# A hybrid encoder layer with retrieval on one core: gates from contiguous one-hots, output and query by pairs of tiles, and other tiles taken densely

## The chip, the cores and the metric

The kernel runs on one core of a Trainium2 chip. The metric is the device time of one execution in microseconds; runs are compared by their medians. Engines are named as in the profile: PE is TensorE, PEld its weight loads, DVE VectorE, ACT ScalarE, POOL GpSimd (it issues the gathers), SP SyncE (it issues the other transfers).

## The reference, cut to what matters

One layer over 1024 tokens of 1024 channels: modulation from a conditioning vector, an input projection, chunked band attention (8 heads of 64) beside a gated delta rule (4 heads of 128, a state carried from chunk to chunk), an output projection, and a retrieval of single-neuron experts. The last part decides most of the time:

```
qry = rms_norm((hb @ w_query).reshape(128, 8, 256), query_gain)
s1, s2 = scores of the two halves of qry against 128 sub-keys each
v1, i1 = top_k(s1, 16); v2, i2 = top_k(s2, 16)
top_s, pos = top_k(v1[..., :, None] + v2[..., None, :], 16)
experts = i1 * 128 + i2 at pos              # 8 heads x 16 of 16384 experts
gates = softmax(top_s)
act = gelu(einsum(expert_down[experts], hb))
y = einsum(gates * act, expert_up[experts])
```

## The kernel before, in words

The 1024 tokens are eight tiles of 128. For each tile the front does a projection (`project`, lane P, for groups of one or two tiles, `GROUPS`), the delta rule (`delta`, lane D, one tile behind the other by the state), attention (`attention`, lane M), the output projection with the second norm, the query and its top 16 (`output`, lane O), the choice of experts (`choose`, lane R) and, for dense tiles, the gates (`gates_dense`, lane G). A scheduler orders the instructions of each engine by the lanes' priorities (`PRI`, `STEP` a tile, `SHIFT` by hand) and by its own idea of time; each engine then runs its list in order. What a lane may hold in flight is set by its rings of buffers (`RINGS`, `WBUFS`) and PSUM banks (`BANKS`).

The experts are served in two ways. For a **dense** tile (`DENSE`) every expert is computed: the gates are spread to a table of 128 x 128 experts for each token (`gates_dense` builds one-hots of the two keys and multiplies them on PE), and `dense` runs over all experts in 32 steps of four blocks, with products split in a high and a low part. For a **sparse** tile (`SPARSE`) the 128 chosen rows of each token are gathered: `down` issues 128 indirect gathers of 128 x 1024 and a dot product on DVE for each (L893, L895), `up` another 128 with a multiply-add (L907, L912). Each gather goes into a row buffer of a ring: three in the front (`NROW`), and four more when the dense stage's pools are opened (`NMORE`). `FRONT` says behind which tile's front work a sparse tile's rows are put in, `LATE` which tiles' rows go in beside the dense stage; rows have a low priority. The dense stage's pools take the memory of the front's lanes.

Of the kernel before, what the change touches and what calls it, by code (L numbers as in the profile page):

```python
# [50 lines left out]
BANKS = {"P": 2, "D": 2, "M": 1, "O": 1}  # L51
RINGS = {'P': 4, 'D': 12, 'M': 4, 'O': 3, 'R': 2, 'G': 6}
XBUFS = {'P': 1, 'O': 1}
# [3 lines left out]
SPREAD = {('P', 0): 'PR', ('P', 1): 'PR', ('O', 6): 'ORR', ('D', 0): 'DDO'}  # L57
# [5 lines left out]
SHIFT = {('P', 7): -4000, ('P', 5): 5000, ('R', 0): -5000, ('O', 0): -3000, ('O', 7): -13000, ('M', 5): -5000, ('D', 1): 2000, ('O', 6): 11000, ('P', 0): 5000, ('D', 3): -2000, ('R', 3): -3000, ('R', 4): -10000, ('D', 6): 3000, ('M', 4): 2000, ('D', 5): 5000, ('R', 6): 10000, ('G', 5): 1000, ('R', 1): -10000}  # L63
OLANE = {7: 'P'}
ONV = ''
# [57 lines left out]
def hybrid_layer(ctx, tc, a, out):  # L123
# [385 lines left out]
    def attention(t, mixT):  # L509
# [3 lines left out]
        for p in range(4):  # L513
# [9 lines left out]
            for hh in range(2):  # L523
# [3 lines left out]
                for lo, hi, bias in ((m0, 3, farm[:, min(m0, 2) * P:]), (max(m0, 3), 5, near[:, hh, (max(m0, 3) - 3) * P:])):  # L527
# [159 lines left out]
    def output(t, mixT):  # L687
        x = x4("x1")
        SP.dma_start(x, a["x"][rows_(t)])
        for nb in range(2):  # L690
            ps = natural(mixT, [t], "w_out", nb)[t]
            cs = slice(nb * 512, (nb + 1) * 512)
            tmp = rg()
            gate_row(tmp, 0, cs)
            V.tensor_tensor(tmp, ps, tmp, OP.mult)
            V.tensor_tensor(x[:, cs], x[:, cs], tmp, OP.add)
            yield
        h2T = lt([P, KD, P], F, "h2T", 1, "h2T" if cur[0] == "O" else "hT")
        SP.dma_start(x1d[rows_(t)], x)
        norm_T(x, h2T, 0, a2, sh2)  # L700
        yield
        if t in DENSE:
            SP.dma_start(h2Td[DENSE.index(t)], h2T)
        else:
            h2 = x4("h2")
            for q in range(2):
                ps = mm()
                for j in range(4):
                    PE.transpose(ps[:, j * P:(j + 1) * P], h2T[:, 4 * q + j, :], ident)
                A_.activation(h2[:, q * 512:(q + 1) * 512], ps, AF.Copy)  # L710
            SP.dma_start(h2d[rows_(t)], h2)
        yield
        nb = 2 if cur[0] == "O" else 1
        v12 = lt([P, 16, TOPK], F, "v12", nb)
        i12 = lt([P, 16, TOPK], U32, "i12", nb)
        ssq = lt([P, PH], F, "ssq", nb)
        for blk in range(4):
            (_, _, ps), = transposed(h2T, P, "peer_w_query", blk, 4)
            q, sq = rg(), rg()
            A_.activation(sq, ps, AF.Square)  # L720
            for c in range(2):
                A_.activation(q.rearrange("p (a c n) -> p c a n", c=2, n=P)[:, c],
                              ps.rearrange("p (a c n) -> p c a n", c=2, n=P)[:, c], AF.Copy, scale=qgain[:, c:c + 1])
            yield
            pq = mm()
            for cc in range(4):
                PE.matmul(pq[:, cc // 2:cc // 2 + 1], sq[:, cc * P:(cc + 1) * P], ones_col, start=(cc % 2 == 0),
                          stop=(cc % 2 == 1), skip_group_check=True)
            V.tensor_copy(ssq[:, 2 * blk:2 * blk + 2], pq[:, 0:2])
            ps = mm()  # L730
            for cc in range(4):
                PE.matmul(ps[:, cc * P:(cc + 1) * P], q[:, cc * P:(cc + 1) * P], skT[:, cc % 2, :], start=True, stop=True,
                          skip_group_check=True)
            sc_ = copy(ps)
            for cc in range(4):
                top16(sc_[:, cc * P:(cc + 1) * P], P, v12[:, 4 * blk + cc, :], i12[:, 4 * blk + cc, :])
                yield
        TOP[t] = v12, i12, ssq
# [11 lines left out]
    def choose(t):  # L750
# [39 lines left out]
        e12 = lt([P, 2, PH, TOPK], F, "e12", 2)  # L790
# [37 lines left out]
        ROUTE[t] = (idx, idf.rearrange("p h s -> p (h s)"), gt.rearrange("p h s -> p (h s)"))  # L828
        yield


# [238 lines left out]
```

## Time and profile before

| | |
|---|---|
| median of 3 runs | 3556.13 us (3547.57 to 3564.26) |
| the profiled execution | 3552.79 us |
| its span, first to last instruction | 3551.0 us |
| mean granted TensorE clock | 0.914 of full speed |
| busy: PE, DVE, POOL, ACT | 3131.2, 2797.2, 1281.6, 1029.7 us |
| moved by DMA | 1029.12 MB, 290 GB/s |

The busy times are unions of what an engine had in work; matmuls overlap each other, so a busy PE isn't a full one. Shares over the span mix three stages with different limits, so stretches are read apart below. Nothing runs beside another core.

### The profile page before, as it was taken

Reading aid. Unit: us, or ns where it says so; the run is one execution under the profiler, and the core shown is the slowest. Engines: PE = TensorE matmul, PEld = TensorE weight load, DVE = VectorE, ACT = ScalarE, POOL = GpSimd, SP = SyncE. Lnnn points to the kernel's source line nnn. Section 1 sums busy time; section 2 is a strip of 40 time slices with the busy share of each in tenths; the row PEclk is TensorE's granted clock in tenths of the full one; section 3 lists DMA queues with packets and bytes.
Section 4 is the critical chain, followed back from the end, with each engine's and each line's share of the span. In section 5 each row is a group of like instructions: output and inputs, shape, how many; then the busy total and the mean of one; then the engine's idle time right before and its main releaser. Section 6 shows DMA issues by size and latency. Waiting matters only on the chain.

```text
span 3551.0 us, 46244 instructions
## 1 busy us (share of the span) xinstructions
PE 3131.2 (88%) x16220; PEld 2603.9 (73%) x16220; DVE 2797.2 (79%) x6626; ACT 1029.7 (29%) x1809; POOL 1281.6 (36%) x1028
## 2 busy tenths in 40 slices
PE   6888789899989899999856999999989999999990
PEld 4678678788778788788755777777777777777870
DVE  3346577877876886656688888999989888999899
ACT  2233243234423343232212322222222222222220
POOL 0000333222222330000232446666655655665455
PEclk9999889998889899987878999999999999999995
DMA  8865789887787897543787989999999998999889
GB/s 280 280 215 170 256 298 315 298 284 246 241 289 244 274 323 247 196 144 133 268 283 254 313 301 342 338 355 355 355 333 351 340 334 318 352 362 367 311 276 356
DMA packets 382602, 1029.12 MB, mean 290 GB/s; under 512 B 34576, under 2 KB 135312, under 8 KB 382368
## 3 DMA queue, kind: packets, MB, share of 16 engines
q0 software_dynamic: 147456, 536.94, 42.1%
q1 hardware_dynamic: 234912, 489.23, 40.3%
q8 instruction: 127, 2.08, 0.2%
q14 instruction: 107, 0.88, 0.1%
HBM read 964.16 MB, written 61.87 MB: 289 GB/s over the span
## 4 chain that ended last, share of the span: by engine, by line
DVE 14%; PE 12%; DMA 10%; issue 10%; POOL 4%; ACT 1%; DVEq 0%; POOLq 0%; ACTq 0%; SPq 0%
PE yc L993 5%; PE at L971 5%; DMA g<-gd 4%; DVE row L895 4%; DVE y L912 3%; POOL row L893 3%; DMA row<-in_peer_expert_down_dram,idx 3%; DMA rawd<-_peer_expert_down_t_dram 2%; DVE ulo L953 1%; DVE yacc L998 1%; DVE dlo L953 1%; POOL row L907 1%; DVE gl L977 1%; DMA row<-in_peer_expert_up_dram,idx 1%; PE mm L364 1%
## 5 line engine op out<-in xcount | busy, mean ns | idle before, releaser
L893 POOL DMA_INDIRECT row<-in_peer_expert_down_dram,idx x512 | 646.5, 1263 | 1489.1 <-DVE idx L827 411.3
L907 POOL DMA_INDIRECT row<-in_peer_expert_up_dram,idx x512 | 634.9, 1240 | 754.8 <-DVE y L912 314.3
L895 DVE CUSTOM_DVE_ANT_0 row<-row,h2a 128x1024 f32<-128x1024 f32 x512 | 620.2, 1217 | 122.0 <-DMA row<-in_peer_expert_down_dram,idx 121.3
L912 DVE SCALAR_TENSOR_TENSOR y<-row,act,y 128x1024 f32<-128x1024 f32 x508 | 649.4, 1278 | 11.6 <-DMA row<-in_peer_expert_up_dram,idx 8.6
L993 PE MATMUL yc<-uhi,whi 128*128 128x512 f32 x1024 | 397.2, 400 | 32.2 <-ACT whi L980 24.4
L993 PE MATMUL yc<-ulo,whi 128*128 128x512 f32 x1024 | 402.0, 396 | 14.6 <-DVE ulo L953 14.5
L993 PE MATMUL yc<-uhi,wlo 128*128 128x512 f32 x1024 | 370.9, 396 | 7.1 <-DVE wlo L981 6.9
L971 PE MATMUL at<-hhi,dhi 128*128 128x512 f32 x1024 | 269.2, 405 | 72.6 <-ACT dhi L952 46.4
L971 PEld LDWEIGHTS at<-hhi,dhi 128*128 128x128 f32 x1024 | 195.3, 194 | 128.3 <-ACT dhi L952 88.0
L364 PE MATMUL mm<-h2T,w 128*128 128x128 f32 x2048 | 272.6, 292 | 17.1 <-DMA w<-in_peer_w_query_dram 7.3
L364 PEld LDWEIGHTS mm<-h2T,w 128*128 128x128 f32 x2048 | 265.3, 207 | 26.6 <-DMA w<-in_peer_w_query_dram 8.5
L870 PE MATMUL mm<-rg 128*128 128x128 f16 x1024 | 263.1, 411 | 7.5 <-ACT stg L873 6.3
L993 PEld LDWEIGHTS yc<-uhi,whi 128*128 128x128 f32 x1024 | 195.9, 192 | 85.8 <-ACT whi L980 32.3
L971 PE MATMUL at<-hlo,dhi 128*128 128x512 f32 x1024 | 258.7, 394 | 0.0
L971 PE MATMUL at<-hhi,dlo 128*128 128x512 f32 x1024 | 255.1, 389 | 0.0
L350 PE MATMUL mm<-w,hT 128*128 128x256 f32 x1024 | 243.2, 389 | 1.4 <-ACT raw L441 0.9
L993 PEld LDWEIGHTS yc<-ulo,whi 128*128 128x128 f32 x1024 | 195.7, 191 | 58.7 <-DVE ulo L953 18.2
L993 PEld LDWEIGHTS yc<-uhi,wlo 128*128 128x128 f32 x1024 | 195.3, 191 | 50.2 <-DVE wlo L981 9.7
L971 PEld LDWEIGHTS at<-hlo,dhi 128*128 128x128 f32 x1024 | 196.6, 192 | 42.1
L971 PEld LDWEIGHTS at<-hhi,dlo 128*128 128x128 f32 x1024 | 192.3, 188 | 40.0
L350 PEld LDWEIGHTS mm<-w,hT 128*128 128x128 f32 x1024 | 194.7, 196 | 28.9 <-ACT raw L441 1.1
L870 PEld LDWEIGHTS <-rg 128*128 128x128 f16 x1024 | 146.8, 147 | 78.1 <-issue 8.0
(294 smaller groups left out, 4914.9 us busy)
## 6 DMA issues: line engine op xcount, KB each, us to landing
w<-in_w_in_dram SPq DMA_DIRECT2D x140, 512.0 KB
w<-in_peer_w_query_dram SPq DMA_DIRECT2D x128, 512.0 KB
rawd<-_peer_expert_down_t_dram SPq DMA_DIRECT2D x128, 512.0 KB
rawu<-in_peer_expert_up_dram SPq DMA_DIRECT2D x128, 512.0 KB
w<-in_w_out_dram SPq DMA_DIRECT2D x64, 512.0 KB
gd<-stg SPq DMA_DIRECT2D x64, 512.0 KB
g<-gd SPq DMA_DIRECT2D x32, 1024.0 KB
w<-in_w_ada_dram SPq DMA_DIRECT2D x48, 512.0 KB
```

The source lines that it names most:

```text
L350: PE.matmul(ps[t][:, hf * 256:hf * 256 + 256], hT[:, k, tt * P:(tt + 1) * P], w[k], start=(k == 0), stop=(k == KD - 1), skip_group_check=True)
L364: PE.matmul(ps[:, (c % per) * W:(c % per + 1) * W], w[k][:, (c % 2) * P:(c % 2 + 1) * P], hT[:, k, :W], start=(k == 0), stop=(k == KD - 1) ...
L870: PE.matmul(ps[:, j * P:(j + 1) * P], w[n][:, :, 4 * h + j], oh1[:, :, 4 * h + j], start=(n == 0), stop=(n == GN - 1), skip_group_check=True)
L893: G.indirect_dma_start(out=r, out_offset=None, in_=a["peer_expert_down"], in_offset=bass.IndirectOffsetOnAxis(ap=idx[:, j:j + 1], axis=0))
L895: V.tensor_tensor_reduce(r, r, h2, 1.0, 0.0, OP.mult, OP.add, accum_out=act[:, j:j + 1])
L907: G.indirect_dma_start(out=row, out_offset=None, in_=a["peer_expert_up"], in_offset=bass.IndirectOffsetOnAxis(ap=idx[:, j:j + 1], axis=0))
L912: V.scalar_tensor_tensor(y, row, w[:, j:j + 1], y, op0=OP.mult, op1=OP.add)
L953: V.tensor_tensor(lo, x, hi.bitcast(F), OP.subtract)
L971: PE.matmul(ps, l[:, k, :], r[:, k, :], start=(n == 0), stop=(n == 3 * KD - 1))
L977: V.tensor_tensor(gq, gq, gt[q][:, :, (s % 2) * SCN + c, :], OP.mult)
L993: PE.matmul(ps, l[:, ts_], r[:, cs], start=(m == 0), stop=(m == 3 * SCN - 1))
L998: V.tensor_tensor(yacc[:, n, cs], yacc[:, n, cs], ps, OP.add)
```

## The change

Five things, in one edit. (1) The dense tiles are 2 to 5 instead of 1 to 4, so the sparse ones are 0, 1, 6 and 7; rows of tiles 0 and 1 go into the front, rows of 6 and 7 beside the dense stage (before: 0 in the front, 5 to 7 in `LATE`). (2) `GROUPS` are four pairs, and `output` works on a pair: both tiles share each load of w_out and peer_w_query, and the query's matmuls are 256 columns wide. (3) The gates' one-hots lie token by token in memory instead of eight tokens side by side, and the weighting by the gate moves from DVE (one multiply over eight tokens) to ACT (a scaled copy for each token and part). (4) A query block's attention scores are one matmul over up to three key blocks. (5) The level masks and `iota_n` take less memory, lanes D and O get a second bank, and the hand-set shifts are gone.

```diff
-DENSE = (1, 2, 3, 4)
-FRONT = {0: [('d', 0), ('u', 0)]}
-LATE = [('d', 5), ('u', 5, 1), ('d', 6), ('u', 6, 1), ('d', 7), ('u', 7)]
+DENSE = (2, 3, 4, 5)
+FRONT = {0: [('d', 0)], 1: [('u', 0, 1), ('d', 1), ('u', 1)]}
+LATE = [('d', 6), ('u', 6, 1), ('d', 7), ('u', 7)]
...
 NROW = 3
 NMORE = 4
...
-XBUFS = {'P': 1, 'O': 1}
+XBUFS = {'P': 1, 'O': 2}
...
-BANKS = dict(P=2,D=1,M=1,O=1,R=1)
-GN = 2
+BANKS = dict(P=2, D=2, M=1, O=2, R=1)
 GQ = 8
-GT = mybir.dt.bfloat16 if GN == 3 else BF
-GROUPS = [[0], [1, 2], [3, 4], [5, 6], [7]]
+GROUPS = [[0, 1], [2, 3], [4, 5], [6, 7]]
...
-                    for m in range(lo, hi):
-                        PE.matmul(ps[:, (m - lo) * P:(m - lo + 1) * P], kv[hp, 0, :], kv[hp, 1 + m, :], start=True,
-                                  stop=True, skip_group_check=True)
+                    PE.matmul(ps[:, :(hi - lo) * P], kv[hp, 0, :],
+                              kv[hp, 1 + lo:1 + hi, :].rearrange("p m c -> p (m c)"), start=True, stop=True,
+                              skip_group_check=True)
...
-    def output(t, mixT):
+    def output(tiles, mixT):
+        W = len(tiles) * P
...
-            (_, _, ps), = transposed(h2T, P, "peer_w_query", blk, 4)
+            for c0, per, ps in transposed(h2T, W, "peer_w_query", blk, 4):
...
-                oh1, oh2 = hot(), hot()
-                V.tensor_tensor(oh1, iota_n, spread_(0), OP.is_equal)
-                V.tensor_tensor(oh2, iota_n, spread_(1), OP.is_equal)
-                w = [hot() for _ in range(GN - 1)] + [oh2]
-                for n in range(GN):
-                    V.tensor_tensor(w[n], oh2, spread_(2 + n), OP.mult)
+                oh1, oh2, whi, wlo = (rg((P, GQ * P), BF).rearrange("p (n i) -> p n i", n=GQ) for _ in range(4))
+                for oh, key in ((oh1, 0), (oh2, 1)):
+                    V.tensor_tensor(oh, iota_n[:, None, :].to_broadcast([P, GQ, P]),
+                                    keys[:, key, n0:n0 + GQ, None].to_broadcast([P, GQ, P]), OP.is_equal)
                 for h in range(GQ // 4):
                     ps = mm()
                     for j in range(4):
-                        for n in range(GN):
-                            PE.matmul(ps[:, j * P:(j + 1) * P], w[n][:, :, 4 * h + j], oh1[:, :, 4 * h + j],
-                                      start=(n == 0), stop=(n == GN - 1), skip_group_check=True)
+                        n = 4 * h + j
+                        for m, w in enumerate((whi, wlo)):
+                            A_.activation(w[:, n, :], oh2[:, n, :], AF.Copy, scale=parts[:, m, n0 + n:n0 + n + 1])
+                            PE.matmul(ps[:, j * P:(j + 1) * P], w[:, n, :], oh1[:, n, :], start=(m == 0),
+                                      stop=(m == 1), skip_group_check=True)
...
-            mixT = pools_["O"].tile([P, KD, P], F, name="mixT", tag="mixT", bufs=2)
-            lane("D", when("D", t), run, delta(t, mixT), tile_=t)
-            lane("M", when("M", t), run, attention(t, mixT), tile_=t)
-            with tc.issue_after(first_loads) if t == 0 else ExitStack():
-                lane(OLANE.get(t, "O"), when("O", t), run, output(t, mixT), tile_=t)
+        with tc.issue_after(first_loads) if n == 0 else ExitStack():
+            lane("O", when("O", g[0]), run, output(g, mixT), tile_=g[0])
```

What the scheduler made of it is seen at three places. The first is GpSimd's list from its first gather, before (L893 gathers down rows, L907 up rows; a count stands at the end of a row):

```order
L893 DMA row<-in_peer_expert_down_dram,idx 128x1024 x128
L907 DMA row<-in_peer_expert_up_dram,idx 128x1024 x128
L893 DMA row<-in_peer_expert_down_dram,idx 128x1024 x56
L907 DMA row<-in_peer_expert_up_dram,idx 128x1024
L893 DMA row<-in_peer_expert_down_dram,idx 128x1024
```

And the same list of the change, from where the up rows of tile 1 stand; ahead of it are tile 0's 128 down rows, and then its up rows and tile 1's down rows by turns, 128 of each:

```order
L907 DMA row<-in_peer_expert_up_dram,idx 128x1024 x128
L893 DMA row<-in_peer_expert_down_dram,idx 128x1024 x100
L907 DMA row<-in_peer_expert_up_dram,idx 128x1024
L893 DMA row<-in_peer_expert_down_dram,idx 128x1024 x5
L907 DMA row<-in_peer_expert_up_dram,idx 128x1024
```

Where tile 0's 256 gathers were followed by tile 5's, now 512 of tiles 0 and 1 come ahead of any of tile 6.

The second place is VectorE's list at the start of the dense stage, before (hlo is the low part of the dense tiles' input; L742 to L746 are top 16 searches of the last tile):

```order
L743 MAX_INDEX pos<-tv,rg 128x8
L742 MAX tv<-rg 128x8
L772 COPY d_15265<-i_15263 128x8
L745 MAX tv<-wk 128x8
L773 TENSOR_TENSOR d_15265<-i_15263 128x8x15
L944 TENSOR_TENSOR hlo<-hraw,hhi 128x8x128
```

And of the change, from the last up rows of tile 1 (L912) to their gate and residual (L919, L920); hlo stands some fifty rows further down, and no row pass of tiles 0 and 1 behind it:

```order
L912 SCALAR_TENSOR_TENSOR y<-row,act,y 128x1024
L790 SCALAR_TENSOR_TENSOR b__15793<-pf 128x128
L805 TENSOR_TENSOR rg<-pf,tab_280 128x1024
L787 CAST m_15791<-pw 128x128
L805 TENSOR_TENSOR rg<-pf,tab_280 128x1024
L827 TENSOR_REDUCE s_15868<-gt 128x8
L309 TENSOR_SCALAR s_15996<-ssq 128x8
L912 SCALAR_TENSOR_TENSOR y<-row,act,y 128x1024
L810 TENSOR_TENSOR rg<-rg,d_15786 128x256 x2
```

The third place is the gates of one tile, before, on VectorE (L861 and L862 compare for the one-hots, L865 weights them, L912 is a row pass, L624 one of the delta rule):

```order
L912 SCALAR_TENSOR_TENSOR y<-row,act,y 128x1024 x2
L861 TENSOR_TENSOR rg<-iota_n,gparts 128x1024
L862 TENSOR_TENSOR rg<-iota_n,gparts 128x1024
L729 COPY ssq<-mm 128x2
L865 TENSOR_TENSOR rg<-rg,gparts 128x1024
L309 TENSOR_SCALAR s_8504<-ssq 128x8
L624 TENSOR_TENSOR rg<-rg,kc 128x512
L865 TENSOR_TENSOR rg<-rg,gparts 128x1024
```

And of the change on ScalarE, where each L869 is one token's scaled one-hot, L873 takes four tokens' products out of PSUM, and L538 and L579 belong to attention and the delta rule:

```order
L869 ACTIVATE rg<-rg,gparts 128x128 x15
L538 ACT_TABLE_LOAD
L538 ACTIVATE sx,s_10682<-sx,s_10690 128x640
L873 ACTIVATE stg<-mm 128x128x4
L538 ACTIVATE sx,s_10682<-sx,s_10700 128x640
L869 ACTIVATE rg<-rg,gparts 128x128 x2
L873 ACTIVATE stg<-mm 128x128x4
L869 ACTIVATE rg<-rg,gparts 128x128 x6
```

The weighting has left VectorE's list; 1024 such copies stand in ScalarE's, between the chains of attention and the delta rule, and TensorE's gate matmuls each read one of them.

## Rows read from the trace of the kernel before

**Rows 1.** Stretches: time, then busy us (x instructions) by engine, clock, DMA.

```profile
core 0: us, PE busy (x) PEld busy (x) DVE busy (x) ACT busy (x) POOL busy (x), PEclk, DMA share, GB/s
0.00:371.00 371.00, 310.74 (x2010) 252.28 (x2011) 168.91 (x745) 113.75 (x255) 3.35 (x7) 0.93 0.68 229
371.00:812.00 441.00, 394.41 (x2325) 347.52 (x2325) 333.58 (x1082) 153.87 (x323) 132.72 (x127) 0.91 0.85 297
...
1711.00:1884.00 173.00, 124.01 (x811) 115.61 (x810) 131.86 (x519) 35.10 (x78) 62.20 (x55) 0.79 0.82 281
0.00:1915.00 1915.00, 1683.88 (x10076) 1435.47 (x10076) 1314.90 (x4639) 616.47 (x1286) 345.28 (x319) 0.88 0.74 252
1915.00:3465.00 1550.00, 1447.36 (x6144) 1168.47 (x6144) 1404.69 (x1925) 413.28 (x524) 889.28 (x664) 0.98 0.93 333
3465.00:3551.00 86.00, 0.00 (x0) 0.00 (x0) 77.58 (x64) 0.00 (x0) 47.00 (x46) 0.50 0.93 361
```

**Rows 2.** DVE's row passes alone in such stretches: busy us (x passes).

```profile
core 0: us, DVE busy (x), PEclk, DMA share, GB/s
371.00:812.00 441.00, 154.96 (x128) 0.91 0.85 297
...
0.00:1915.00 1915.00, 386.60 (x312) 0.88 0.74 252
1915.00:3465.00 1550.00, 807.02 (x661) 0.98 0.93 333
3465.00:3551.00 86.00, 66.00 (x52) 0.50 0.93 361
```

**Rows 3.** Timeline from 1763 us, start and duration: DVE's down rows, one gather.

```profile
1763.69 1.21 DVE L895 CUSTOM_DVE_ANT_0 row<-row,h2a 128x1024 f32<-128x1024 f32 x1
...
1765.17 0.94 POOL L893 DMA_INDIRECT row<-in_peer_expert_down_dram,idx  x1 [3.64 <-DVE v L745]
...
1772.99 1.22 DVE L895 CUSTOM_DVE_ANT_0 row<-row,h2a 128x1024 f32<-128x1024 f32 x1 [1.03 <-DMA row<-in_peer_expert_down_dram,idx]
```

**Rows 4.** Row tiles in 1711 to 1884 us; gathers and waits in 371 to 812.

```profile
L895 DVE CUSTOM_DVE_ANT_0 row<-row,h2a x56: 1198/1220/1227, 1710.6 to 1883.4; 128x1024 f32<-128x1024 f32 x56
...
DMA to landing us min/median/max: 4.1/7.0/10.0
...
  DVE act L895: 131.6, 50
...
DMA to landing us min/median/max: 4.2/7.2/10.6
...
DVE row L895 <- DMA row<-in_peer_expert_down_dram,idx: 67.0, 39, 5.5
```

**Rows 5.** By line: key scores (PE) in 300 to 345, 560 to 665; idx.

```profile
L732 PE MATMUL mm<-peer_sub_keys,rg x16: 273/275/276, 309.0 to 328.3; 128*128 128x128 f32 x16
...
L732 PE MATMUL mm<-peer_sub_keys,rg x32: 272/275/421, 562.2 to 659.6; 128*128 128x128 f32 x32
...
L827 DVE CAST idx<-idf x4: 205/217/220, 365.1 to 1931.6; 128x128 int32<-128x128 f32 x4
```

**Rows 6.** PE's timeline: fp32 products at 56, dense ones at 2300, dense start.

```profile
58.80 2.48 PE L364 MATMUL mm<-hT,w 128*128 128x128 f32 x20
...
2299.91 0.39 PE L993 MATMUL yc<-uhi,wlo 128*128 128x512 f32 x1
2300.14 0.39 PE L993 MATMUL yc<-uhi,whi 128*128 128x512 f32 x1
...
1915.70 0.80 PE L971 MATMUL at<-hhi,dhi 128*128 128x512 f32 x1 [26.03 <-DVE hlo L944]
```

**Rows 7.** Groups by line and form: busy, mean ns, idle before.

```profile
L870 PE MATMUL mm<-rg 128*128 128x128 f16 x1024 | 263.1, 411 | 7.5 <-ACT stg L873 6.3 <-DVE rg L865 0.7 <-DVE s L314 0.3
...
L865 DVE TENSOR_TENSOR rg<-rg,gparts 128x1024 f16<-128x1024 f16 x128 | 86.9, 683 | 0.5
...
L796 DVE TENSOR_TENSOR rg<-pf,tab 128x1024 f16<-128x1024 f16 x16 | 19.4, 1215 | 0.0
...
L670 ACT ACTIVATE rg<-rg,e 128x128 f32<-128x128 f32 x96 | 33.4, 394 | 11.4 <-PE mm L327 10.2 <-DVE s L314 1.2
```

**Rows 8.** Timeline of the end.

```profile
3542.36 4.62 DVE L1006 TENSOR_TENSOR x1c<-x1c,yacc 128x1024 f32<-128x1024 f32 x4
```

More of the change, by code (lines that the diff above doesn't have):

```diff
@@ L684, in delta_side @@
         yield
-    def output(t, mixT):
-        x = x4("x1")
-        SP.dma_start(x, a["x"][rows_(t)])
+    def output(tiles, mixT):
+        W = len(tiles) * P
+        xs = []
+        for t in tiles:
+            xs.append(x4("x1"))
+            SP.dma_start(xs[-1], a["x"][rows_(t)])
         for nb in range(2):
-            ps = natural(mixT, [t], "w_out", nb)[t]
+            ps_ = natural(mixT, tiles, "w_out", nb)
             cs = slice(nb * 512, (nb + 1) * 512)
[L693 to L696, printed above, removed]
-            yield
[L698 to L706, printed above, removed]
-                ps = mm()
[L708 to L717, printed above, removed]
-            (_, _, ps), = transposed(h2T, P, "peer_w_query", blk, 4)
[L719 to L738, printed above, removed]
@@ new lines, in output @@
+            g1 = rg()
+            gate_row(g1, 0, cs)
+            for t, x in zip(tiles, xs):
+                tmp = rg()
+                V.tensor_tensor(tmp, ps_[t], g1, OP.mult)
+                V.tensor_tensor(x[:, cs], x[:, cs], tmp, OP.add)
+            yield
+        h2T = lt([P, KD, 256], F, "h2T", 1)
+        for tt, (t, x) in enumerate(zip(tiles, xs)):
+            SP.dma_start(x1d[rows_(t)], x)
+            norm_T(x, h2T, tt, a2, sh2)
+            yield
+            own = h2T[:, :, tt * P:(tt + 1) * P]
+            if t in DENSE:
+                SP.dma_start(h2Td[DENSE.index(t)], own)
+            else:
+                h2 = x4("h2")
+                for q in range(2):
+                    ps = mm()
+                    for j in range(4):
+                        PE.transpose(ps[:, j * P:(j + 1) * P], own[:, 4 * q + j, :], ident)
+                    A_.activation(h2[:, q * 512:(q + 1) * 512], ps, AF.Copy)
+                SP.dma_start(h2d[rows_(t)], h2)
+            yield
+            TOP[t] = (lt([P, 16, TOPK], F, "v12", 2), lt([P, 16, TOPK], U32, "i12", 2), lt([P, PH], F, "ssq", 2))
@@ L823, in choose @@
             return
-        idf = keep.tile([P, PH, TOPK], F, name="idf", tag="idf")
+        idf = lt([P, PH, TOPK], F, "idf", 1)
         V.scalar_tensor_tensor(idf, e12[:, 0], 128.0, e12[:, 1], op0=OP.mult, op1=OP.add)
@@ L1039, in hybrid_layer @@
             lane("P", ADAP, run, ada_rest())
-        for t in g:
-            mixT = pools_["O"].tile([P, KD, P], F, name="mixT", tag="mixT", bufs=2)
-            lane("D", when("D", t), run, delta(t, mixT), tile_=t)
-            lane("M", when("M", t), run, attention(t, mixT), tile_=t)
-            with tc.issue_after(first_loads) if t == 0 else ExitStack():
-                lane(OLANE.get(t, "O"), when("O", t), run, output(t, mixT), tile_=t)
+        mixT = pools_["O"].tile([P, KD, 256], F, name="mixT", tag="mixT", bufs=1)
+        for tt, t in enumerate(g):
+            own = mixT[:, :, tt * P:(tt + 1) * P]
+            lane("D", when("D", t), run, delta(t, own), tile_=t)
+            lane("M", when("M", t), run, attention(t, own), tile_=t)
+        with tc.issue_after(first_loads) if n == 0 else ExitStack():
+            lane("O", when("O", g[0]), run, output(g, mixT), tile_=g[0])
+        for t in g:
             lane("R", when("R", t), run, choose(t), tile_=t)
```

78 lines of the change are left out of this document (49 added, 29 removed).

## The prediction

> **What bounds the kernel now.** I read the busy time by stretches first, then the sparse row passes in the same stretches, then what one row waits for, then the dense stage and the tail. The program falls into three parts [rows 1]: a front of 1915 us (projections, delta rule, attention, output and query, routing, gates), a dense stage from 1915 to 3465 us, and a tail of 86 us. In the dense stage TensorE is the bound: it has 6144 matmuls that follow each other at 0.227 us [rows 6], so 1395 us at the least of 1550; VectorE is busy 1405 of the 1550 and DMA 93% of it, both close behind. In the tail TensorE is idle, and 52 row passes are worked off [rows 1, 2].
>
> The front is tied to TensorE (1684 of 1915 us busy), with VectorE at 1315. The sparse tiles' row passes lie in it as filling. Their count is what matters here: 312 of the 1024 stand ahead of the dense stage [rows 2]. One row is a gather of 512 KB into one of three buffers (NROW) and one VectorE pass. The reader is to see in [rows 3] how one buffer turns: a pass starts at 1763.69 and lasts 1.21, the buffer's next gather is issued at 1765.17, and the pass on it starts at 1772.99, held up by its DMA: 9.3 us, in which each of the three buffers turns once. A gather lands a median 7.0 to 7.2 us after its issue [rows 4]. So three rows take some 1.2 + 0.3 to the issue (the two starts in [rows 3] are 1.48 apart) + 7.0 + about 0.4 to the next pass = 8.9 us, 2.97 us a row, however idle the engines are. What the stretches show: 128 down rows in 441 us, 3.45 a row, with VectorE busy 76% and TensorE 89%; 56 rows in 173 us, 3.09 a row, with VectorE 76% and TensorE 72% [rows 1, 2]. In the dense stage four more buffers are there, and 661 rows take 1550 us, 2.34 a row, beside everything else.
>
> **The change, part by part.**
>
> *Four sparse tiles, now two and two.* Ahead of the dense stage 512 rows stand in VectorE's order instead of 312, and hlo, which the first dense matmul needs, stands behind them all. All 512 go through the same three buffers, since NROW is unchanged and the four further buffers come only with the dense pools; two streams that alternate (up of tile 0, down of tile 1) share them.
>
> When can the first row go? The key scores of tile 0 end at 328 us and of tile 1 at 660, and tile 0's idx stands at 365 [rows 5], 37 us behind. Weighing each matmul in the orders by its columns at the trace's pace, TensorE has 309 us of work up to the first of these and 570 to the second; in the changed order the pair 0, 1 has its last key scores at 463. Interpolated: 328 + (463 - 309) / (570 - 309) x 332 = 524 us; with 37 us, and 14 us for a second tile's selections in between, the first row is at 575 us (540 to 610).
>
> Then 512 rows. Bounds: 2.97 us each by the cycle above, 3.45 by the d-row stretch. I take 3.15, nearest to the 56 rows, because the changed front has less TensorE work beside its rows, as that stretch had: 512 x 3.15 = 1613 us. From the last row of a stretch to the first dense matmul it was 1883.4 to 1915.7 [rows 4, 6], 32 us; I take 30. The dense stage then starts at 575 + 1613 + 30 = 2218 us, 303 later.
>
> *Does VectorE have room for that?* 200 more rows at 1.24 us (386.6 / 312, [rows 2]) are 248 us. The gates' multiplications go, 128 x 0.683 = -87 us; the one-hot compares now read a key that repeats along the inner axis, which L796 also does at the same size, so 128 x (1.215 - 0.683) = +68 if they cost now what L865 does at the same size [rows 7]. VectorE's work before the dense stage goes from 1315 to about 1545 us, some 240 of it ahead of the first row (169 by 371 us, [rows 1], and a second tile's searches): 1305 in 1643 us, 79%. It is not the bound, but near it. A rule speaks against this edit: the Trainium skill (VectorE: DVE Perf Modes, What auto-detection actually checks) has the faster 16-bit mode only where every tensor steps by one. By it the compare falls back to one element a cycle, which is the 1.215 of L796; were the compare to stay at 0.683, the sum here would be 68 us lower in VectorE work and the forecast the same.
>
> *Gates.* 1024 TensorE matmuls on strided one-hots show 263 us of busy time for 1024 x 0.411 overlapping [rows 7]; contiguous ones can't cost more than that nor less than nothing. I take 80 us left (a fp32 product of 128 columns is two records at about 0.12 us, [rows 6], and this is one record). ScalarE gets 1024 scalings of 128 x 128, at 0.35 to 0.39 us (busy and mean of L670) some 360 us, on an engine that was busy 616 of 1915. So TensorE loses up to 183 us and ScalarE goes to about 45% of the longer front. Cover for all of this is the wait for rows; without it the front would be up to 183 us shorter.
>
> *Pairs and joined scores.* Query matmuls are half as many at double width, so their columns stay; the 480 score records of 128 columns become 224 of up to 384. Weight loads fall by 28 + 64 + 32 transfers of 512 KB, 62 MB against 105 MB more of rows; the DMA share of the front is 0.74 [rows 1]. More banks for the D and O lanes take some waits off. I put all of these at nothing, since the rows hide them; uncovered they are worth 0 to 60 us.
>
> *Dense stage.* The order has 512 rows left for the first 23 of 32 steps, at 22 a step as now, and none in the last nine. With rows a step takes 1550 / 32 = 48.4 us, without at best 192 x 0.227 = 43.6: nine steps x 4.8, less some for a first step with more down rows, -35 us: 1515. In the tail no rows are left: the four last additions of 4.6 us [rows 8], the products of as many elements ahead of them and the stores behind, some 15 us instead of 86.
>
> Sum: 2218 + 1515 + 15 = 3748 us of span, and 1.8 us outside it as now (3552.8 against 3551.0) gives **3750 us**, 197 above that execution's time and 194 above the median of 3556.1.
>
> **Rivals.**
>
> *Rows keep up, VectorE is the bound.* If gathers land soon enough, the front runs at VectorE's pace: 1305 / 0.9 = 1450 us behind the first row, dense at 575 + 1450 + 5 = 2030, total 3562, no change. For it: in the d-row stretch its own waits for rows are only 67 us [rows 4]. Against it: GpSimd sat idle for 132 us of that stretch until such a pass freed a buffer [rows 4], so the ring of three was what turned, and the changed order puts less other work between two rows.
>
> *Faster.* The same with VectorE packed to 97% (the dense stage has 1405 of 1550, 91%): 1305 / 0.97 = 1345, dense at 1925, total 3457. It decides where three rows take under 8.3 us: (3551 - 1530 - 605) / 512 = 2.77 us a row. A page gives a price that would do it. The Trainium skill (DMA: Bandwidth & Descriptors, Anatomy of one DMA — SWDGE (gpsimd) path) has 2.0 us plus the bytes at 436 GB/s, 3.2 us for 512 KB, as an estimate from that page; by it the three-row cycle is about 5.1 us and rows are never the bound. The trace disagrees: the shortest landing in [rows 4] is 4.1 us and the median 7.0, so I give this little.
>
> *Gates stall TensorE.* Every gate matmul now waits for its own ScalarE scaling, in TensorE's queue, with delta, attention and projections behind it. If the order has too little between, 1024 x 0.36 = 369 us of TensorE replace 263, and later tiles' chains slip by about 100 us beyond the rows: 3850.
>
> **How the numbers follow.** Forecast (rows' three buffers set the front) 0.60; gates stall 0.11; VectorE bound 0.15; faster 0.14. The forecast alone spans 540 + 1520 + 20 to 610 + 1766 + 30 for the dense start, 3612 to 3938. The range reaches to the case of no change and leaves out the faster one and the top: 3550 to 3900. About half a per cent (18 us) is what a measurement of this kernel can tell from no change. Faster by more: 0.16 (the faster case and a little of the VectorE one); within: 0.08; slower: 0.76.
>
> **What would show it.** First row pass near 575 us; the 512th near 2190; 3.0 to 3.5 us a row between, GpSimd's gathers waiting for row passes and VectorE's passes waiting for landings; compares at 1.2 us; gate matmuls far shorter than 0.41 us; steps of 43 to 45 us in the last nine; a tail of about 15 us. It is wrong if landings in the longer front fall to 5 us or less, if VectorE is over 90% busy behind 575 us, or if the first row comes before 450.

## The result, and the profile after

The changed kernel takes 3683.9 us (median of 4 runs, 3669.15 to 3686.31) against 3555.5 for the kernel before (median of 4, one run more than stood above): a ratio of 1.037 [1.034, 1.040], slower. The profiled execution took 3682.53 us, its span is 3680.8 us. The forecast was 3750 us, in a range of 3550 to 3900.

The stretches of the changed kernel, cut at the first row, the last row ahead of the dense stage and the first dense matmul (columns as in [rows 1]), answer to [rows 1]:

```profile
core 0: us, PE busy (x) PEld busy (x) DVE busy (x) ACT busy (x) POOL busy (x), PEclk, DMA share, GB/s
552.00:930.00 378.00, 313.54 (x1497) 260.30 (x1496) 275.42 (x776) 127.33 (x268) 146.62 (x130) 0.81 0.84 283
930.00:1700.00 770.00, 559.82 (x3145) 468.10 (x3143) 651.27 (x1912) 360.34 (x946) 290.12 (x251) 0.81 0.82 276
1700.00:2101.00 401.00, 226.75 (x1221) 180.09 (x1221) 325.35 (x783) 230.70 (x682) 157.80 (x128) 0.66 0.78 261
0.00:2132.00 2132.00, 1575.55 (x8604) 1299.54 (x8604) 1532.38 (x4716) 892.38 (x2278) 602.40 (x521) 0.81 0.73 245
...
3506.00:3593.00 87.00, 87.00 (x385) 72.07 (x384) 40.58 (x57) 26.03 (x32) 0.00 (x0) 1.00 0.37 110
```

VectorE's row passes alone in the first three of them, as in [rows 2]:

```profile
552.00:930.00 378.00, 158.22 (x130) 0.81 0.84 283
930.00:1700.00 770.00, 315.43 (x253) 0.81 0.82 276
1700.00:2101.00 401.00, 163.19 (x128) 0.66 0.78 261
```

The front was 1915 us and is now 2132. TensorE has less work in it than before (1576 against 1684 us) and waits for a quarter of it; VectorE has 1532 us of 2132, 72%. Rows run at 378/130 = 2.91, 770/253 = 3.04 and 401/128 = 3.13 us each. So they get no faster in the last 401 us, where TensorE is busy for only 57% and VectorE for 81%. The chain that ended last, from the first row to the dense start, by line:

```profile
by line: DMA row<-in_peer_expert_up_dram,idx 28.7%; DMA row<-in_peer_expert_down_dram,idx 17.2%; DVE y L912 8.7%; issue 8.7%; DVE row L895 6.5%; DVE rg L862 3.4%; POOL row L893 2.6%; DVE wk L753 1.3%; POOL row L907 1.2%; PE mm L350 1.1%; DV
```

Gathers (28.7 + 17.2), row passes (8.7 + 6.5) and their issues (2.6 + 1.2) are 65% of it. VectorE's own waits for rows, from 552 to 1700 us (total us, times, longest):

```profile
DVE row L895 <- DMA row<-in_peer_expert_down_dram,idx: 141.0, 90, 5.7
DVE y L912 <- DMA row<-in_peer_expert_up_dram,idx: 45.5, 46, 3.0
```

They were 67 us in 441 before [rows 4], now 187 in 1148: about the same share, 16% for 15%. What the gates became, by line and form (before: [rows 7]):

```profile
L870 PE MATMUL mm<-rg 128*128 128x128 f16 x1024 | 108.9, 266 | 82.4 <-ACT stg L873 58.7 <-DVE s L313 13.9 <-ACT rg L869 5.0
...
L862 DVE TENSOR_TENSOR rg<-iota_n,gkeys 128x1024 f16<-128x1024 f16 x128 | 150.9, 1218 | 1.8 <-PE mm L870 1.8
...
L869 ACT ACTIVATE rg<-rg,gparts 128x128 f16<-128x128 f16 x1024 | 317.7, 394 | 133.2 <-DVE rg L862 87.2
```

The end of the program, as in [rows 8], now holds no rows; VectorE's last operations behind the last product are these:

```profile
3674.42 1.22 DVE L1005 TENSOR_TENSOR yacc<-yacc,g2c 128x1024 f32<-128x1024 f32 x1
3675.68 1.23 DVE L1006 TENSOR_TENSOR x1c<-x1c,yacc 128x1024 f32<-128x1024 f32 x1
```

Behind the dense start the changed kernel gains: 3681 - 2132 = 1549 us against 3551 - 1915 = 1636. The whole loss is ahead of it: 217 us, less 87, is the 130 us of the span. The dense start is not quite the end of the front's work, though. The first 192 dense matmuls, one step's worth, take 46 us in the kernel before and 86 here, with VectorE busy for 75 of them (the first row is of the kernel before):

```profile
1915.70:1961.50 45.80, 45.65 (x192) 37.14 (x193) 39.47 (x81) 18.21 (x24) 17.07 (x14) 0.96 0.73 261
2132.30:2218.00 85.70, 54.39 (x192) 41.62 (x193) 75.30 (x154) 19.36 (x26) 47.61 (x40) 0.77 0.84 297
```

### The profile page after: what moved, and what is told of

The parts are those of the page before. It is cut to its first block, busy times and chain, and to the rows that moved or that the text cites. A ratio compares the mean times of both kernels' runs of the same rounds, so it can differ in the third digit from the quotient of the medians.

```text
span 3680.8 us, 43839 instructions
## 1 busy us (share of the span) xinstructions
PE 3017.8 (82%) x14748; PEld 2470.0 (67%) x14748; DVE 2783.0 (76%) x6444; ACT 1307.8 (36%) x2801; POOL 1284.5 (35%) x1028
## 4 chain that ended last, share of the span: by engine, by line
PE 31%; DVE 28%; DMA 28%; issue 9%; POOL 2%; ACT 2%; SPq 0%; DVEq 0%; POOLq 0%; ACTq 0%
DMA row<-in_peer_expert_up_dram,idx 12%; PE yc L993 9%; PE at L971 9%; DMA row<-in_peer_expert_down_dram,idx 9%; DVE y L912 7%; DVE row L895 6%; PE mm L364 4%; DMA g<-gd 4%; PE mm L350 3%; POOL row L893 2%; DVE rg L862 1%; DVE ulo L953 1%; DVE dlo L953 1%; DMA w<-in_w_ada_dram 1%; DVE gl L977 1%
## 5 line engine op out<-in xcount | busy, mean ns | idle before, releaser
L893 POOL DMA_INDIRECT row<-in_peer_expert_down_dram,idx x512 | 650.1, 1270 | 1282.5 <-DVE tv L751 569.9
L907 POOL DMA_INDIRECT row<-in_peer_expert_up_dram,idx x512 | 634.1, 1239 | 718.1 <-DVE y L912 207.1
L912 DVE SCALAR_TENSOR_TENSOR y<-row,act,y 128x1024 f32<-128x1024 f32 x508 | 650.4, 1280 | 118.3 <-DMA row<-in_peer_expert_up_dram,idx 114.8
L869 ACT ACTIVATE rg<-rg,gparts 128x128 f16<-128x128 f16 x1024 | 317.7, 394 | 133.2 <-DVE rg L862 87.2
L364 PE MATMUL mm<-h2T,w 128*128 128x256 f32 x1024 | 238.1, 392 | 25.7 <-DVE ssq L735 20.7
L998 DVE TENSOR_TENSOR yacc<-yacc,yc 128x512 f32<-128x512 f32 x248 | 162.9, 681 | 125.6 <-PE yc L993 125.5
L364 PEld LDWEIGHTS mm<-h2T,w 128*128 128x128 f32 x1024 | 199.2, 197 | 57.9 <-DVE ssq L735 22.8
L952 ACT ACTIVATE uhi<-rawu 128x1024 fp32r<-128x1024 f32 x128 | 131.9, 1052 | 276.7 <-PE yc L993 217.5
```

Of the source, the lines that this page charges most:

```text
L364: PE.matmul(ps[:, (c % per) * W:(c % per + 1) * W], w[k][:, (c % 2) * P:(c % 2 + 1) * P], hT[:, k, :W], start=(k == 0), stop=(k == KD - 1) ...
L869: A_.activation(w[:, n, :], oh2[:, n, :], AF.Copy, scale=parts[:, m, n0 + n:n0 + n + 1])
L893: G.indirect_dma_start(out=r, out_offset=None, in_=a["peer_expert_down"], in_offset=bass.IndirectOffsetOnAxis(ap=idx[:, j:j + 1], axis=0))
L907: G.indirect_dma_start(out=row, out_offset=None, in_=a["peer_expert_up"], in_offset=bass.IndirectOffsetOnAxis(ap=idx[:, j:j + 1], axis=0))
L912: V.scalar_tensor_tensor(y, row, w[:, j:j + 1], y, op0=OP.mult, op1=OP.add)
L952: A_.activation(hi, x, AF.Copy)
```

## The experiments

The theory was that the row ring (three buffers, one turn in about 9 us, 512 rows) sets the start of the dense stage. The rivals were VectorE's work, the new gates, and the chain of the last pair of tiles. The table has for each kernel, from its profiled execution, the first row pass, the mean us a row over the first 256, the row passes ahead of the first dense matmul, and when that came. Labels with a_ start from the changed kernel, those with b_ from the kernel before, and those with n_ from the kernel before with the new gates. Ratios are to the kernel before, run on the same chip; each time is the median of four runs or more, that of `a_ring2` of two.

| kernel | median us | ratio | first row | us a row | rows ahead | dense start |
|---|---|---|---|---|---|---|
| before | 3555 | 1 | 371 | 3.97 | 312 | 1916 |
| after | 3684 | 1.037 | 552 | 3.00 | 515 | 2132 |
| a_ring4 | 3609 | 1.017 [1.014, 1.020] | 552 | 2.59 | 519 | 2026 |
| a_gates4 | 3648 | 1.028 [1.025, 1.031] | 556 | 2.96 | 515 | 2116 |
| a_split | 3619 | 1.020 [1.017, 1.023] | 550 | 3.22 | 312 | 1981 |
| b_split | 3665 | 1.034 [1.029, 1.038] | 372 | 3.50 | 476 | 2122 |
| b_newgates | 3441 | 0.970 [0.966, 0.975] | 372 | 3.55 | 312 | 1803 |
| a_oldgates | 3689 | 1.040 [1.035, 1.044] | 551 | 3.00 | 505 | 2137 |
| b_ring4 | 3562 | 1.003 [1.000, 1.006] | 370 | 3.28 | 320 | 1918 |
| b_mix4 | 3616 | 1.021 [1.015, 1.026] | 377 | 3.04 | 388 | 2014 |
| a_ring2 | 3754 | 1.057 [1.050, 1.064] | 549 | 3.96 | 385 | 2080 |
| n_split | 3602 | 1.015 [1.010, 1.020] | 370 | 3.29 | 505 | 2054 |
| n_noshift | 3492 | 0.982 [0.978, 0.987] | 376 | 3.62 | 312 | 1860 |
| n_joined | 3480 | 0.981 [0.976, 0.985] | 350 | 3.34 | 312 | 1821 |

The 515 are the 512 of tiles 0 and 1 and three of tile 6.

**A fourth row buffer, and its control.** The memory for it comes from the gates' ring, so the control has the small gates' ring alone.

```diff
-NROW = 3
+NROW = 4
-RINGS = {'P': 4, 'D': 12, 'M': 4, 'O': 3, 'R': 2, 'G': 6}
+RINGS = {'P': 4, 'D': 12, 'M': 4, 'O': 3, 'R': 2, 'G': 4}
```

> The change with four row buffers in the front instead of three; for the memory the gates' ring is four instead of six. Ring theory (three buffers, each turning in about 9 us, set the front's 512 rows): a row falls from 3.03 us to about 2.6, where VectorE becomes the bound, the dense stage starts near 1920 instead of 2132, the total is near 3480. Rival 1 (gate matmuls that wait for ScalarE, and the low clock with it, set the front): start and total stay at 2132 and 3684 within 20 us, rows are only further ahead. Rival 2 (VectorE is the bound already): under 60 us gained.

The control has the second line only:

> The control for it: the change with the gates' ring at four and three row buffers. Ring theory: 3684 within 20 us, dense start near 2132, since gates are covered by the rows. Rival 1 (gates set the front): with a shorter ring ScalarE and TensorE overlap less, 30 to 100 us slower.

Against its control the fourth buffer brings the dense start from 2116 to 2026 us and the row from 2.96 to 2.59 us. It is faster by 40 us in all, with intervals that don't touch. The ring theory's 1920 and 3480 are missed by over 100 us each, and 40 us lies within the "under 60" of the rival that VectorE is the bound already. The same chain, from the first row to the dense start, by line, the control first:

```profile
by line: DMA row<-in_peer_expert_up_dram,idx 22.3%; DMA row<-in_peer_expert_down_dram,idx 19.4%; DVE y L912 10.1%; issue 9.7%; DVE row L895 8.1%; DVE rg L862 4.4%; POOL row L893 3.1%; DVE wk L753 1.4%; PE mm L350 1.2%; DVE rg L805 1.2%; DVE
by line: DMA row<-in_peer_expert_up_dram,idx 13.6%; DMA row<-in_peer_expert_down_dram,idx 13.5%; issue 11.2%; DVE y L912 9.4%; DVE row L895 8.3%; DVE rg L862 5.1%; POOL row L893 2.9%; PE mm L364 2.8%; POOL row L907 2.2%; PE mm L350 1.8%; DV
```

Gathers fall from 46% of the chain in the change, and 42% in the control, to 27%: the ring was the limit, and with one more buffer it is one limit among several. What is next is seen in the front from the first row on, and in its last 101 us:

```profile
552.00:2026.00 1474.00, 1112.13 (x5792) 887.83 (x5791) 1271.42 (x3624) 705.55 (x1829) 625.07 (x519) 0.79 0.83 290
...
1925.00:2026.00 101.00, 51.20 (x268) 36.03 (x266) 87.98 (x398) 64.89 (x187) 10.77 (x10) 0.62 0.40 152
```

And the last up rows of tile 1 in both kernels, the control first (durations in ns, then the first and last start):

```profile
L912 DVE SCALAR_TENSOR_TENSOR y<-row,act,y x61: 1265/1283/1318, 1900.1 to 2072.6; 128x1024 f32<-128x1024 f32 x61
```

```profile
L912 DVE SCALAR_TENSOR_TENSOR y<-row,act,y x46: 1264/1280/1317, 1799.6 to 1923.9; 128x1024 f32<-128x1024 f32 x46
```

The last row of tiles 0 and 1 comes 149 us sooner (1923.9 for 2072.6), but 59 of them are given back: behind it the gates and the key scores of the last tiles are still under way for 101 us, with VectorE busy 88 of these and TensorE 51. Over the whole stretch VectorE is busy 1271 of 1474 us, 86%. Of the 90 us at the dense start another 44 are lost right behind it: 72 gate matmuls are still to come there, and the first dense step takes 103 us where the control has 59.

```profile
L870 PE MATMUL mm<-rg x72: 219/229/311, 2030.8 to 2083.5; 128*128 128x128 f16 x72
...
2026.00:2129.00 103.00, 60.25 (x263) 45.65 (x263) 88.47 (x166) 43.18 (x100) 58.18 (x42) 0.72 0.89 311
...
2116.00:2175.00 59.00, 49.32 (x192) 39.09 (x192) 51.27 (x123) 16.94 (x22) 21.81 (x15) 0.88 0.88 292
```

The last row is the control's. The control itself is 36 us faster than the change, where no difference over 20 was expected: 16 us of it stand ahead of the dense start, and the first dense step is 27 us shorter (59 for 86). Why a shorter ring for the gates does that stays open. TensorE's gates wait longer in it for the scaled copies, 77.7 us from the first row to the dense start, where the change has 5.0:

```profile
PE mm L870 <- ACT rg L869: 77.7, 27, 6.6
```

**Two row buffers.**

```diff
-NROW = 3
+NROW = 2
```

> The change with two row buffers in the front instead of three; the scheduler then puts 384 rows ahead of the dense stage instead of 512. Ring theory: one buffer turns in the same 9 us, so a row takes 4.4 to 4.7 us instead of 3.03, the 384 rows take 1690 to 1800 us from 552, the dense stage starts at 2270 to 2380, total 3800 to 3950. Rival (VectorE's work between the rows sets their pace): 3.0 to 3.4 us a row, dense start under 2000.

A row takes 3.96 instead of 3.00 us, as the theory's sign has it; 4.4 to 4.7 was expected, by a turn of 9 us for each buffer. With two buffers the turn is 2 x 3.96 = 7.9 us. Part of the turn is the time from a gather's issue to its landing, here in the summary of the row tile on GpSimd's side:

```profile
DMA to landing us min/median/max: 3.9/5.3/11.3
```

With at most two gathers in flight they land sooner than with three in the kernel before: a median 5.2 us for down rows and 5.5 for up rows, against 7.2 [rows 4] and 6.1. Ahead of the dense start only 385 rows stand: the scheduler moved the others into the dense stage, so that the dense start fell to 2080 and the end came later. The expectation had counted on that (384 rows), so its 2270 to 2380 is missed by the price of a row alone: 549 + 385 x 3.96 = 2074. The total of 3754 is below its 3800 to 3950 too.

**The change with the old assignment, and the old kernel with the new one.** The first takes three lines of the diff back (the second makes the same edit in the kernel before):

```diff
-DENSE = (2, 3, 4, 5)
-FRONT = {0: [('d', 0)], 1: [('u', 0, 1), ('d', 1), ('u', 1)]}
-LATE = [('d', 6), ('u', 6, 1), ('d', 7), ('u', 7)]
+DENSE = (1, 2, 3, 4)
+FRONT = {0: [('d', 0), ('u', 0)]}
+LATE = [('d', 5), ('u', 5, 1), ('d', 6), ('u', 6, 1), ('d', 7), ('u', 7)]
```

> The change with the dense and sparse tiles of before (1 to 4 dense, one sparse tile in the front, three late), all else as changed. 312 rows stand ahead of the dense stage. Ring theory: the front isn't bound by rows any more, it shows what gates, pairs and joined scores are worth: dense start 1780 to 1880, dense stage and tail as before (1636), total 3420 to 3520, faster than before. Rival 1 (gates on ScalarE or pairs are what made the change slow): dense start stays over 2000, total 3640 to 3700.

> The kernel before with only the tiles' assignment of the change (2 to 5 dense, 0 and 1 in the front, 6 and 7 late). 472 rows stand ahead of the dense stage, and the first can go at 371 us. Ring theory: rows need at least 371 + 472 x 3.1 = 1834 us, no more than the front's 1915, but together with TensorE's 1684 us of work the front comes to 1960 to 2060, with 1565 behind it 3530 to 3630: slower by 0 to 2%. Rival 1 (the assignment costs nothing, gates and pairs do): 1915 + 1550 = 3465, 2.5% faster than before.

The assignment alone makes the old kernel nearly as slow as the whole change (3665, dense start +206). That is more than the theory had: a dense start of 1960 to 2060 and 3530 to 3630 us were expected, and a row takes 3.50 us there, not 3.1. But without the assignment the change is still 65 us later to the dense stage than before (1981), where 1780 to 1880 was expected, and takes 3619 us, between the two theories' totals. So something else in the change costs there. It stands at the end of the front, in four stretches of `a_split`:

```profile
1467.00:1620.00 153.00, 137.82 (x936) 119.98 (x936) 103.86 (x493) 106.83 (x298) 0.00 (x0) 0.94 0.42 140
1620.00:1700.00 80.00, 40.77 (x186) 27.66 (x187) 67.21 (x234) 47.40 (x146) 18.40 (x14) 0.54 0.41 134
1700.00:1800.00 100.00, 49.75 (x254) 36.14 (x253) 66.75 (x112) 60.50 (x182) 47.78 (x37) 0.52 0.78 259
1800.00:1981.00 181.00, 109.98 (x524) 92.97 (x524) 99.61 (x567) 35.59 (x74) 8.45 (x9) 0.78 0.40 139
```

Rows are a small part of it: of the 56 of tile 5, none is passed up to 1620, 37 between 1700 and 1800, and 9 behind that; the kernel before and `b_newgates` below have the same 56. TensorE is busy half of 1620 to 1800. The last gates and the last key scores of this kernel, by line, in the stretch behind 1620:

```profile
L870 PE MATMUL mm<-rg x256: 216/311/314, 1633.2 to 1796.2; 128*128 128x128 f16 x128
...
L739 PE MATMUL mm<-peer_sub_keys,rg x64: 275/275/356, 1868.3 to 1937.1; 128*128 128x128 f32 x64
```

**The gates alone, both ways.** The new gates in the kernel before, and the old ones in the change (there with a ring of five for them):

```diff
-                V.tensor_tensor(oh1, iota_n, spread_(0), OP.is_equal)
-                V.tensor_tensor(oh2, iota_n, spread_(1), OP.is_equal)
-                w = [hot() for _ in range(GN - 1)] + [oh2]
-                for n in range(GN):
-                    V.tensor_tensor(w[n], oh2, spread_(2 + n), OP.mult)
+                for oh, key in ((oh1, 0), (oh2, 1)):
+                    V.tensor_tensor(oh, iota_n[:, None, :].to_broadcast([P, GQ, P]),
+                                    keys[:, key, n0:n0 + GQ, None].to_broadcast([P, GQ, P]), OP.is_equal)
...
+                            A_.activation(w[:, n, :], oh2[:, n, :], AF.Copy, scale=parts[:, m, n0 + n:n0 + n + 1])
```

> The kernel before with only the gates of the change (contiguous one-hots, weighting on ScalarE). The version with before's tiles and all else changed started its dense stage at 1981 us against 1916. Theory A (the gates' waits for ScalarE cost that): dense start 1950 to 2000, total 3590 to 3640. Theory B (pairs cost it, in the last pair's output): TensorE is relieved by some 150 us of gate matmuls, dense start 1860 to 1920, total 3490 to 3555.

> The change with the gates of before (strided one-hots, weighting on VectorE; the gates' ring is five for the memory). Ring theory (three row buffers set the front): the 512 rows cover the gates, so dense start 2132 and total 3684 within 30 us. Theory A (gates on ScalarE slow the front): dense start 2050 to 2090, total 3600 to 3640.

In the change the gates make no difference (2137 and 2132), as the ring theory had it; in the kernel before they are worth 113 us of the dense start. That is beyond both theories' ranges (1803, where the faster one had 1860 to 1920), and 3441 us is the fastest time of this study, 3.0% below before. Its gates and its last key scores:

```profile
L861 PE MATMUL mm<-rg 128*128 128x128 f16 x1024 | 97.1, 235 | 15.3 <-ACT stg L864 14.8
...
L861 PE MATMUL mm<-rg x1024: 216/219/314, 742.4 to 1569.0; 128*128 128x128 f16 x171
...
L732 PE MATMUL mm<-peer_sub_keys,rg x64: 275/275/519, 1634.6 to 1749.5; 128*128 128x128 f32 x64
```

TensorE's gates go from 263.1 to 97.1 us, its wait for ScalarE is 15 us, and its work in the front from 1684 to 1513: in a front tied to TensorE the 166 us come out as 113. What makes `a_split`'s dense start 178 us later than this one arises late, for the delta rule's state is finished at about the same time in both (`a_split` first):

```profile
L649 DVE SCALAR_TENSOR_TENSOR state<-state,e,mm x32: 326/343/349, 214.7 to 1596.9; 128x128 f32<-128x128 f32 x32
...
L649 DVE SCALAR_TENSOR_TENSOR state<-state,e,mm x32: 327/342/349, 172.1 to 1604.1; 128x128 f32<-128x128 f32 x32
```

**Four buffers in the kernel before.** The edit of the first experiment:

> The kernel before with four row buffers in the front (the gates' ring four for the memory). Before has one sparse tile there, whose 256 rows end at 1384 us, 530 ahead of the dense stage, so the ring matters for the 56 rows of tile 5 alone. Ring theory: dense start 1880 to 1920, total 3500 to 3560, the same or 1% faster. Were the fourth buffer itself good (more rows at any place), 60 us or more.

No difference beyond half a per cent (1.003). A row does get faster, 3.28 us for 3.97, and the dense start doesn't move (1918): with 312 rows the ring is no limit there, though its buffers turn in 9 us there too [rows 3].

**Half of the rows moved back.** In the kernel before, with four buffers: the changed dense tiles, but tile 1's up rows beside the dense stage.

```diff
+DENSE = (2, 3, 4, 5)
+FRONT = {0: [('d', 0), ('u', 0)], 1: [('d', 1)]}
+LATE = [('u', 1, 1), ('d', 6), ('u', 6, 1), ('d', 7), ('u', 7)]
```

> The kernel before with the tiles of the change, but tile 1's up rows moved to the dense stage (385 rows ahead of it), and four row buffers. Ring theory: rows need 371 + 385 x 2.6 = 1370 us, under the front's 1916, so what is left is VectorE's 90 us more: dense start 1930 to 2000; 639 rows behind it at 22 a step last 29 of 32 steps, so no tail: 1550 + 15; total 3495 to 3565. Rival (rows in the front cost the front whatever the ring, as in the version with only the assignment, 206 us for 164 rows): dense start 2005, total 3570 to 3590.

The ring's 1930 to 2000 is missed, the rival's side is right: 2014 us for its 2005; the total of 3616 is above both. From the end of the last delta rule, at 1655, to the dense start only 3 rows are passed, and yet it takes 360 us. Three stretches of it, and the gates in them by line:

```profile
1655.00:1750.00 95.00, 86.92 (x499) 72.66 (x498) 40.83 (x156) 23.99 (x49) 0.00 (x0) 0.80 0.48 166
1750.00:1850.00 100.00, 59.62 (x246) 33.30 (x245) 40.04 (x96) 17.45 (x30) 0.00 (x0) 0.53 0.16 63
1850.00:2014.00 164.00, 78.28 (x447) 65.33 (x447) 76.32 (x412) 23.16 (x44) 8.14 (x7) 0.69 0.44 149
...
L870 PE MATMUL mm<-rg x381: 387/413/438, 1654.7 to 1868.0; 128*128 128x128 f16 x191
```

Tile 5 is dense now, and its gates can only be made when its selection is there, so they stand at the end of the front, up to 1868, and the last output and query products share TensorE with them. VectorE and TensorE wait for each other there. Up to the last delta rule nothing is lost: its state is finished at 1629, and at 1672 in `b_ring4` (the last line), which has the same ring and the old assignment.

```profile
DVE rg L862 <- PE mm L870: 92.6, 22, 8.6
...
L649 DVE SCALAR_TENSOR_TENSOR state<-state,e,mm x32: 335/340/347, 174.7 to 1629.1; 128x128 f32<-128x128 f32 x32
...
L649 DVE SCALAR_TENSOR_TENSOR state<-state,e,mm x32: 326/341/348, 171.5 to 1671.5; 128x128 f32<-128x128 f32 x32
```

So the 96 us between their dense starts (1918 and 2014) arise behind the last delta rule.

**The kernel with new gates, plus one part each.** The changed assignment; no hand-set shifts and lanes; joined scores with the wider banks. The diff is that of the second (two entries of SPREAD go with it); the edits of the other two stand above.

```diff
-SHIFT = {('P', 7): -4000, ('P', 5): 5000, ('R', 0): -5000, ('O', 0): -3000, ('O', 7): -13000, ...
-OLANE = {7: 'P'}
+SHIFT = {}
+OLANE = {}
```

> The kernel before with the change's gates and the change's assignment of tiles, but without pairs, joined scores and the lost shifts. The gates alone brought the dense start to 1803, the assignment alone to 2122. Ring theory (512 rows at 3.0 us from the first at 372 set the front): 372 + 501 x 3.0 + 30 = 1905, total 3440 to 3500. Rival (the assignment also puts the gates of the last dense tile behind the last tiles' chains, whatever the rows): 2000 to 2070, total 3540 to 3610.

> The kernel before with the change's gates and without the hand-set shifts (SHIFT empty, OLANE empty, two entries of SPREAD gone), as in the change. It tells what cost 178 us between the version with the gates alone (1803) and the one with all but the assignment (1981). Shifts: dense start 1900 to 1980, total 3540 to 3620. Pairs: 1800 to 1850, total 3440 to 3490.

> The kernel before with the change's gates, joined attention scores and the two further PSUM banks for lanes D and O. Expected by all theories small: dense start 1770 to 1810, total 3400 to 3445, the same as the gates alone or 1% faster; if the scores of up to 384 columns hold up the next lane, 10 to 30 us slower.

The assignment costs 251 us of dense start there (2054). The ring's figure of 1905 is missed and the rival's 2000 to 2070 holds. It doesn't decide between the two, for the rows run on up to the dense start: they begin at 370 us and run at 3.29, not the 3.0 of the expectation, and 370 + 505 x 3.29 = 2031. From 1820 us, behind the last gate, VectorE still waits for them:

```profile
DVE y L903 <- DMA row<-in_peer_expert_up_dram,idx: 58.4, 38, 6.9
```

The shifts are worth 57 us (1860, between the ranges of the two theories). The joined scores with their banks make it 18 us later to the dense stage and 39 us slower in all (3480 and 3441; their intervals of the ratio, [0.976, 0.985] and [0.966, 0.975], all but touch), more than the 10 to 30 us of the worse case expected. The traced execution of that kernel, 3462 us, is the fastest of its four, so the 18 us may be too few.

Put one on the other, the medians divide the change: the gates take 3555 to 3441 us, the assignment 3441 to 3602, and all the rest (pairs, joined scores, banks, lost shifts, smaller buffers) 3602 to 3684; the ratios go 0.970, 1.015, 1.037. That holds in this order only: in the kernel before, the assignment alone costs 110 us (`b_split`), not 161.

## Why the prediction came out as it did

**The ring, right.** The forecast's mechanism is what the changed kernel shows: the chain and the waits agree, a row's price follows the ring's size in both directions, if by less than the theory had, and the gates, 113 us when uncovered, vanish under the rows. The terms, against what was measured:

| term | predicted | measured |
|---|---|---|
| first row | 575 | 552 |
| us a row, 512 rows | 3.15, 1613 | 3.03, 1549 (552 to 2101) |
| last row to the first dense matmul | 30 | 31 |
| dense start | 2218 | 2132 |
| dense stage and tail | 1515 + 15 | 1542 + 7 |
| sum of the span | 3748 | 3681 |

**The mis-sized term is the 3.15 us a row**, 64 us too much. With the first row 23 too late the front comes out 86 too long; the stage and tail behind it, 19 too short, take the error of the sum down to 67, which is luck. It was taken from the row stretch of 56 in [rows 1, 2], 3.09, and moved up; the lower bound of 2.97 by the cycle was nearer. The first row at 552 is an interpolation that held to 23 us. The dense stage is 27 us longer than its term: two steps without rows take the 87 us that two of 43.6 make, with the clock at 1.00, and the excess is in the first step, 86 us for the 46 of the kernel before.

**Gates, half right.** 80 us were left for TensorE; it is 108.9 busy and 82.4 of waits, under the rows. The compares at 1.218 us are the price of L796 [rows 7]. The Trainium skill (VectorE: DVE Perf Modes, What auto-detection actually checks) gives an operation on two tensors its faster 16-bit mode if every tensor is 16-bit and steps by one. The trace agrees: 1.218 us with the key repeated along the inner axis, where L865 at the same size took 0.683. The rival of gates that stall TensorE got no support: with the old gates the time is the same, and in `b_newgates` TensorE's gates wait for ScalarE 15 us in all. In `a_gates4` they wait 78 us for the scaled copies alone, and that kernel is faster than the change.

**The rival of VectorE as the bound** had 2030 for the dense start, if gathers kept up. With four buffers it was 2026, with VectorE at 86% of the stretch for the 90% assumed. The number is near, and yet not proof: the last 101 us of it hold no row of tiles 0 and 1 and belong for the most part to the chain of the last tiles. The landing of 3.2 us that was estimated from the Trainium skill (DMA: Bandwidth & Descriptors, Anatomy of one DMA — SWDGE (gpsimd) path) isn't reached with two gathers in flight either: 3.9 us at the least, 5.3 in the median.

**What the runs contradict is "Pairs and joined scores", put at nothing, and 0 to 60 us uncovered, as a gain; the lost shifts have no term at all.** Under the rows they cost 82 us, 3602 to 3684 (`n_split` and the change). The sum wasn't hurt, since it had the pairs' wait in it as the later first row (370 us in `n_split`, 552 here). Uncovered they cost too. `a_split` has the new gates and yet its dense start is 178 us behind `b_newgates` (1981 and 1803). 57 of these go with the shifts and 18 with the joined scores and banks, if they add up; about 100 are left for the pairs and the buffers that changed with them (one for `e12` instead of two, two for `x1` instead of one). The rows shown above suggest how: with pairs, the selection of tile 4 comes with tile 5's, so its gates stand at 1633 to 1796, where `b_newgates` has its last gate at 1569; and both tiles of the last pair have their key scores at 1868 to 1937, where there the last two tiles had them at 1635 to 1749. No kernel with pairs alone was run, so the 100 us are a remainder, and the order of the stages is their likely cause, not a shown one.

**The assignment costs by two ways, of which the prediction had one.** Rows: the ring. And the last dense tile is now tile 5, one later, so its gates come behind its selection at the end of the front. `b_mix4` shows the second nearly without the first: 3 rows in the last 360 us. How the 206 us of `b_split` divide between the two is not settled.

## What to carry to other kernels

A filler that is cheap by its busy time (1.24 us of VectorE a row) has a second price, the turn of its buffers: multiply the count by turn over buffers, and compare that with the stretch it is to fill, before the filler is moved into it. The turn isn't fixed: here it was 7.9, 9.0 and 10.4 us with two, three and four buffers (2 x 3.96, 3 x 3.00, 4 x 2.59). Look at the first step behind a stage's start as well as at the start: a stage that starts 90 us sooner gained 40. Test the parts of a joined edit apart: one here, the gates, was worth 3.0%, and the others hid it. When work is batched over two tiles, look at the first and the last pair: the first of a pair's two results now comes as late as the second, and what hangs on it starts later (the first row, 552 us for 370) or goes into the stretch where little else is left to do.

## What the runs showed of the hardware

- A 128 x 128 f16 product with both operands strided (a step of eight elements) took 263.1 us for 1024 [rows 7], 0.257 each; with contiguous operands 97.1 us (`b_newgates`), 0.095 each. The change in layout is worth more than half of TensorE's time for them.
- The 512 KB gathers landed later with more row buffers: a median 5.2 us for down rows and 5.5 for up rows with two (`a_ring2`), 7.2 and 6.1 with three (the kernel before). The two kernels differ in other traffic too, so the part of the number in flight isn't shown by itself. A third buffer took a row from 3.96 to 3.00 us, less than half as much again, and a fourth from 2.96 to 2.59.
- TensorE's granted clock was 0.81 over the changed front and 0.88 before [rows 1]. In `a_split` it was 0.94 from 1467 to 1620 us, with TensorE busy 138 of 153 us, and 0.54 and 0.52 from 1620 to 1800, where TensorE waited for half of the time; that is near the lower of its two levels (1.2 of 2.4 GHz). The gate products there took a median 311 ns, in `b_newgates`, with the front at 0.89, 219. In two dense steps without rows, where TensorE never waited, the clock was 1.00.
